# An encoder layer on one core: the issue of two kinds of stores moved from SyncE to GpSimd

## Chip, cores and metric

One Trainium2 chip, one core. The metric is device time in microseconds, the median of three runs of the whole kernel.

## The reference, cut to what matters

One encoder layer is applied to two sequences, of 1024 and 256 tokens, with the same weights. The tokens' projection feeds three groups of heads: a gated delta rule in both directions over chunks of 64 tokens (group A), a retention (group B) and a windowed attention (group C). Their results are gated, joined, projected and normalised. The change lies in group A:

```python
t_mat = jnp.where(strict, a_mat, 0.0) + jnp.eye(CHUNK)
sol = lax.linalg.triangular_solve(t_mat, rhs, left_side=True, lower=True, unit_diagonal=True)
u, w = sol[..., :dv], sol[..., dv:]
...
def step(state, inp):
    u_c, w_c, qk_c, qd_c, kd_c, cd_c = inp
    v_new = u_c - jnp.einsum('bhcd,bhde->bhce', w_c, state)
    o = jnp.einsum('bhcd,bhde->bhce', qd_c, state) + jnp.einsum('bhcs,bhse->bhce', qk_c, v_new)
    state = state * cd_c + jnp.einsum('bhcd,bhce->bhde', kd_c, v_new)
    return state, o
_, o = lax.scan(step, s0, (u, w, qk, q_dec, k_dec, chunk_decay))
```

For each chunk, head and direction a triangular 64 x 64 matrix is inverted, and a scan over the chunks uses the inverse together with the decayed products of queries and keys.

## The kernel before, in words

The 1280 tokens are 10 blocks of 128, or 20 chunks. All products with weights are done in split precision: a float32 value is a high and a low part, and TensorE does three matmuls for each (`dense`, line 86 by its helper).

The work of group A comes in three stages. `prep_stream` goes over the blocks from the last to the first and over both directions `d`, 20 passes in all. A pass loads a small row of decays from `DRD` into `DJ[d]` (line 606, issued by GpSimd), lets TensorE spread it (`sb`), takes exponentials on ScalarE (`ge`), and multiplies on VectorE into two tiles: `at`, the triangular matrix, and `l2`, the three matrices that the scan will use. Both have two buffers. `at` goes to DRAM twice, four transfers into `AGD` (line 631) and one into `ADD_` (line 633); `l2` goes to DRAM with four transfers into `L2D` (one of line 635 for the upper 64 partitions with 2304 B a run, three of line 638 for the lower 64 with 768 B a run; each has 64 x 2 = 128 runs). A small copy on GpSimd (`elc`, line 629) belongs to each pass.

After five blocks `invert(g)` runs, first for g = 1 and, when all blocks are done, for g = 0. It loads the diagonal 32 x 32 blocks of both directions from `AGD` into rows 0 and 1 of the large tile `ot` (line 405), inverts them in place with 61 products and sums on VectorE (the first, over 120 x 2048 elements, needs all that was loaded), sets the diagonals to one (line 427) and stores each direction into `YDD` (line 429): 120 partitions with 32 runs of 128 B each. Both groups use the same two rows of `ot`, so the loads of g = 0 wait until the stores of g = 1 have landed.

`scan_stream` then joins the 32 x 32 blocks to 64 x 64 inverses (`join`: eight of them, five chunks of one direction each; it loads `an` from `ADD_` and `yn` from `YDD`, transposes on VectorE, has two rounds of 32 x 32 matmuls, a product with a mask on GpSimd into `yc`, and a store into `YCD`), and does 20 steps of the scan in both directions (`step`: loads of `l2`, `yc`, `vt` and `kn`, products on GpSimd with beta and with the decay, `sv`). The four joins of g = 1 come first, then two steps, then the four joins of g = 0.

Between all this the products of the other heads are done as filler: `fill` runs the attention stream and the remaining projections beside the scan. The attention begins with a table of positions made by GpSimd (`iota`, line 805, which becomes `bias`), a copy of the queries that ScalarE and GpSimd share (`qh`, line 843), score matmuls into `sb` (two buffers), and a fused sum and maximum on VectorE (`mx`, line 852), which frees the score buffer.

Each engine works through its instructions in order. That order isn't the order of the code: a scheduler sets it from the streams' costs and a timeline of its own, so an edit in one place can move instructions on every engine. SyncE issues all transfers but those of line 265, 374 and 606, which GpSimd issues.

Of the kernel before, what the change touches and what calls it, by code (L numbers as in the profile page):

```python
# [53 lines left out]
def encoder_kernel(ctx: ExitStack, tc: tile.TileContext, I, O, dbg=None, upto=99):  # L54
    nc = tc.nc
    uid = [0]

    def nm(s):
        uid[0] += 1
        return f"{s}_{uid[0]}"  # L60

    def bc(ap, shape):
        return ap.to_broadcast(list(shape))
# [5 lines left out]
    def ps(tag):  # L69
        return psp.tile([128, 512], F32, tag=tag, name=nm(tag))  # L70
# [14 lines left out]
    def mm(out, lhsT, rhs, start=True, stop=True):  # L85
        nc.tensor.matmul(out, lhsT, rhs, start=start, stop=stop)  # L86

    def tt(eng, out, a, b, op):
        eng.tensor_tensor(out=out, in0=a, in1=b, op=op)  # L89
# [30 lines left out]
    ot = big.tile([128, 8, PADW], F32, tag="OT", name="ot")  # L120
# [35 lines left out]
    def acc():  # L156
        wide.append(wide.pop(0))
        return ps(wide[-1])
# [219 lines left out]
    L2D = [[tc.dram_tile([2, 128, 3, 3, 64], F32, name=f"l2d{d}_{b}") for b in range(NB)] for d in range(2)]  # L378
# [3 lines left out]
    YDD = [[tc.dram_tile([120, 32, 32], F32, name=f"yd{d}_{g}") for g in range(2)] for d in range(2)]  # L382
# [5 lines left out]
    T, B = slice(0, 64), slice(64, 128)  # L388
# [11 lines left out]
    IREG = (0, 1)  # L400

    def invert(g):
        for d in range(2):
            with tc.high_priority():
                nc.sync.dma_start(out=ot[0:120, IREG[d], 0:1056].rearrange("p (a b) -> p a b", a=32),
                                  in_=AGD[d][g].rearrange("q c p r x -> (q c p) r x"))

        def two(o0, o1, *dims):

            a = ot[0:120, IREG[0], o0:o0 + 1]  # L410
            return bass.AP(a.tensor, a.offset, [list(a.ap[0]), [(IREG[1] - IREG[0]) * PADW + o1 - o0, 2], *([list(e) for e in dims])])

        y, yd = two(0, 0, (33, 32), (1, 32)), two(32, 32, (0, 32), (33, 32))
        tt(V, y, y, yd, MUL)
        yield 4.2
        for s in range(1, 31):
            na, nb = s, 31 - s
            t3 = two(1056, 1056, (nb, na), (1, nb))

            c = two(s, 33 * (32 - s) + 31 - s, (33, na), (0, nb))  # L420
            r = two(33 * s + s + 1, 33 * (31 - s), (0, na), (1, nb))
            o = two(s + 1, 33 * (32 - s), (33, na), (1, nb))
            tt(V, t3, c, r, MUL)
            tt(V, o, o, t3, ADD)
            if s % 3 == 0:
                yield 2.8
        V.memset(two(0, 0, (34, 32)), 1.0)
        for d in range(2):
            nc.sync.dma_start(out=YDD[d][g], in_=ot[0:120, IREG[d], 0:1056].rearrange("p (a b) -> p a b", a=32)[:, :, 0:32])

    def weave(*run):

# [72 lines left out]
    with tc.tile_pool(name="pa", reuse_waits="tile", bufs=2) as pa:  # L505
# [78 lines left out]
        def prep_stream():  # L584
            for b in reversed(range(NB)):
                tb = slice(b * 128, (b + 1) * 128)
                g3 = []
                for r in range(2):
                    tk = slice(b * 128 + 64 * r, b * 128 + 64 * r + 64)
                    gram = ps("sa")  # L590
                    g3.append(gram[:, 0:384].rearrange("p (q w) -> p q w", q=3))
                    for p in range(3):
                        for h in range(2):
                            rw, o = slice(64 * h, 64 * h + 64), slice(64 - 64 * h, 128 - 64 * h)
                            mm(g3[r][o, p, :].rearrange("p (w t) -> p w t", w=2), kq[rw, p, 0, tk], kq[rw, p, :, tk])
                kt = ps("tr")
                kt3 = kt[:, 0:384].rearrange("p (q w) -> p q w", q=3)
                for p in range(3):
                    nc.tensor.transpose(kt3[:, p, :], kq[:, p, 0, tb], ident)
                kc = pa.tile([128, 2, 3, 64], F32, tag="kc", name=nm("kc"), bufs=1)  # L600
                for r in range(2):
                    for h, rw in ((1, T), (0, B)):
                        S.copy(kc[rw, r], kt3[64 * r:64 * r + 64, :, 64 * h:64 * h + 64])
                for d in range(2):
                    for l in range(2):
                        nc.gpsimd.dma_start(out=DJ[d][2 * l:2 * l + 2], in_=DRD[d][6 * b:6 * b + 6, l].rearrange("n (s t) -> s n t", s=2))
                    ge = pa.tile([128, 2, 2, 3, 64], F32, tag="ge", name=nm("ge"))
                    for i in range(2):
                        pd = ps("sb")
                        mm(pd[:, 0:384], SD[i], DJ[d].rearrange("r n t -> r (n t)"))  # L610
                        if i == 0:
                            for n in range(6):
                                S.activation(out=ge[:, 0, n // 3, n % 3], in_=pd[:, 64 * n:64 * n + 64], func=AF.Exp,
                                             bias=negd[:, d, 2 * b + n // 3, n % 3:n % 3 + 1])
                        else:
                            S.activation(out=ge[:, 1].rearrange("p c q t -> p (c q t)"), in_=pd[:, 0:384], func=AF.Exp)
                    at = pa.tile([128, 2, 3, 2, 33], F32, tag="at", name=nm("at"), bufs=AB)
                    l2 = pa.tile([128, 2, 3, 3, 64], F32, tag="l2", name=nm("l2"))
                    last = 63 if d == 0 else 0
                    gl = ge[:, 0, :, :, last:last + 1]  # L620
                    el = ge[:, 1, :, :, last:last + 1]
                    S.copy(at[:, :, :, :, 32], bc(nbeta[:, d, 2 * b:2 * b + 2, :].unsqueeze(3), [128, 2, 3, 2]))
                    for r in range(2):
                        tt(V, at[:, r, :, :, 0:32], g3[r][:, :, 0:64].rearrange("p q (w t) -> p q w t", w=2),
                           ge[:, 0, r].rearrange("p q (w t) -> p q w t", w=2), MUL)
                        tt(V, l2[:, r, 1], g3[r][:, :, 64:128], ge[:, 0, r], MUL)
                    tt(V, l2[:, :, 2], kc, bc(gl, [128, 2, 3, 64]), MUL)
                    tt(V, l2[:, :, 0], kq[:, :, 1, tb].rearrange("p q (c t) -> p c q t", c=2), ge[:, 1], MUL)
                    G.tensor_copy(elc[:, d, 2 * b:2 * b + 2, :], el.rearrange("p c q t -> p c (q t)"))
                    for q in range(4):  # L630
                        nc.sync.dma_start(out=AGD[d][b // 5][q, 2 * b % 10:2 * b % 10 + 2].rearrange("c p r x -> r (c p) x"),
                                          in_=at[32 * q:32 * q + 32, :, :, q % 2, :].rearrange("r c p x -> r (c p) x"))
                    nc.sync.dma_start(out=ADD_[d][b // 5][2 * b % 10:2 * b % 10 + 2].rearrange("c p q w t -> p c q w t"), in_=at)

                    nc.sync.dma_start(out=L2D[d][b][:, T].rearrange("r p a q t -> p r (a q t)"),
                                      in_=l2[T].rearrange("p r a q t -> p r (a q t)"))
                    for a, a2 in ((0, 1), (1, 0), (2, 2)):
                        nc.sync.dma_start(out=L2D[d][b][:, B, a2].rearrange("r p q t -> p r (q t)"),  # L638
                                          in_=l2[B, :, a].rearrange("p r q t -> p r (q t)"))
                    yield T_PREP / 2  # L640
                if b % 5 == 0:
                    assert "x2" in gone
                    yield from invert(b // 5)


        for _ in spread((10 * T_PREP + 2 * 32.2, prep_stream()), length(PP)):
            pass
# [504 lines left out]
    with tc.tile_pool(name="fw", reuse_waits="tile", bufs=2) as fw:  # L1152
# [21 lines left out]
        for gi in range(2):  # L1174
            c0 = WSEQ[gi][1]
            w = wf.pop()
            for i, b in enumerate(range(NB) if gi else FO):
                tk = slice(b * 128, (b + 1) * 128)
                p = acc()
# [22 lines left out]
        for gi in range(2):  # L1202
# [10 lines left out]
            for b in range(NB):  # L1213
                tk = slice(b * 128, (b + 1) * 128)
                end = gi == 1 and b == NB - 1
                for j, (o, n) in enumerate(((0, 256), (256, 256)) if end else ((0, 512),)):
                    cs = slice(o, o + n)
                    p = acc()
# [50 lines left out]
```

## Time and profile before

| | us |
|---|---|
| median of three runs | 1094.68 (1089.72 to 1098.46) |
| the profiled execution | 1089.4 |
| its span, first to last instruction | 1087.7 |
| TensorE busy | 1012.3 |
| VectorE busy | 626.2 |
| ScalarE busy | 513.4 |
| GpSimd busy | 237.1 |

Between the span and the execution's time lie 1.7 us. Engines are named PE (TensorE; PEld is its loading of weights), DVE (VectorE), ACT (ScalarE), POOL (GpSimd) and SP (SyncE). The time of an instruction that issues a transfer isn't counted as busy. In brackets behind a row stands how long the engine was idle before it and what ended the wait; where several things are waited for, the one that came last by the profile is named, which isn't always the one that mattered.

### The profile page before, as it was taken

Reading aid. Unit: us, or ns where it says so; the run is one execution under the profiler, and the core shown is the slowest. Engines: PE = TensorE matmul, PEld = TensorE weight load, DVE = VectorE, ACT = ScalarE, POOL = GpSimd, SP = SyncE. Lnnn points to the kernel's source line nnn. Section 1 sums busy time; section 2 is a strip of 40 time slices with the busy share of each in tenths; the row PEclk is TensorE's granted clock in tenths of the full one; section 3 lists DMA queues with packets and bytes.
Section 4 is the critical chain, followed back from the end, with each engine's and each line's share of the span. In section 5 each row is a group of like instructions: output and inputs, shape, how many; then the busy total and the mean of one; then the engine's idle time right before and its main releaser. Section 6 shows DMA issues by size and latency. Waiting matters only on the chain.

```text
span 1087.7 us, 20998 instructions
## 1 busy us (share of the span) xinstructions
PE 1012.3 (93%) x7859; PEld 807.6 (74%) x7859; DVE 626.2 (58%) x1303; ACT 513.4 (47%) x1194; POOL 237.1 (22%) x406
## 2 busy tenths in 40 slices
PE   4999999999896799899998999989789999999996
PEld 4768878887785677677776777767567888888885
DVE  6666676754895985555555664575884333412333
ACT  8476779775454554444344322323341121534544
POOL 2001001111212210312323324554451000112311
PEclk9999999999898899999999899989989999999998
DMA  8112112777778336535544434464572530300211
GB/s 258 37 44 69 45 39 58 170 170 180 164 184 173 104 88 131 146 77 137 127 112 109 113 84 116 115 189 113 155 231 65 172 100 1 97 1 10 98 78 77
DMA packets 199071, 120.57 MB, mean 111 GB/s; under 512 B 105906, under 2 KB 180442, under 8 KB 198970
## 3 DMA queue, kind: packets, MB, share of 16 engines
q1 hardware_dynamic: 194074, 118.97, 40.9%
q8 instruction: 62, 1.02, 0.4%
q0 software_dynamic: 4896, 0.27, 0.4%
q14 instruction: 39, 0.32, 0.1%
HBM read 76.26 MB, written 42.91 MB: 110 GB/s over the span
## 4 chain that ended last, share of the span: by engine, by line
PE 72%; DMA 9%; DVE 8%; issue 3%; ACT 3%; SPq 3%; POOL 2%; DVEq 0%; POOLq 0%; ACTq 0%
PE mm L86 42%; PE sa L86 15%; PE sb L86 8%; PE tr L86 4%; DVE ot L984 2%; PE tr L866 1%; DMA xt<-in_x_prompt 1%; DMA ot<-agd 1%; POOL oo L89 1%; DMA oo<-od 1%; DMA agd<-at 1%; DMA raw<-in_w_in 1%; DMA vt<-vtd 1%; PE tr L1191 1%; SPq L638 1%
## 5 line engine op out<-in xcount | busy, mean ns | idle before, releaser
L86 PE MATMUL mm<-xh,whi 128*128 128x512 f32 x720 | 266.7, 370 | 5.0 <-ACT ot L526 1.8
L86 PE MATMUL mm<-xl,whi 128*128 128x512 f32 x720 | 263.3, 366 | 0.0
L86 PE MATMUL mm<-xh,wlo 128*128 128x512 f32 x720 | 263.2, 366 | 0.0
L86 PEld LDWEIGHTS mm<-xh,whi 128*128 128x128 f32 x720 | 138.5, 192 | 30.3 <-ACT ot L526 2.9
L86 PEld LDWEIGHTS mm<-xh,wlo 128*128 128x128 f32 x720 | 138.1, 192 | 22.2 <-issue 1.0
L86 PEld LDWEIGHTS mm<-xl,whi 128*128 128x128 f32 x720 | 138.4, 192 | 20.4 <-issue 0.7
L89 DVE TENSOR_TENSOR ot<-ot 128x1284 f32<-128x1284 f32 (+16 forms) x131 | 85.0, 649 | 28.7 <-ACT ot L102 16.2
L89 DVE TENSOR_TENSOR wlo<-raw,whi 128x1024 fp32r<-128x1024 f32 (+1 forms) x56 | 56.7, 1015 | 39.0 <-ACT whi L149 26.2
L86 PE MATMUL mm<-whi,xh 128*128 128x512 f32 (+1 forms) x168 | 66.6, 398 | 1.3 <-ACT xh L1056 1.3
L86 PE MATMUL mm<-whi,xl 128*128 128x512 f32 (+1 forms) x168 | 66.0, 393 | 0.4 <-DVE xl L89 0.4
L86 PE MATMUL mm<-wlo,xh 128*128 128x512 f32 (+1 forms) x168 | 65.9, 392 | 0.0
L86 PE MATMUL sa<-wlo,xh 128*128 128x512 f32 (+1 forms) x160 | 62.7, 392 | 0.0
L86 PE MATMUL sa<-whi,xl 128*128 128x512 f32 (+1 forms) x160 | 62.6, 391 | 0.0
L86 PE MATMUL sa<-whi,xh 128*128 128x512 f32 (+1 forms) x160 | 62.5, 390 | 0.0
L531 DVE SCALAR_TENSOR_TENSOR ot<-ot,cols 128x1284 f32<-128x1284 f32 x36 | 55.9, 1553 | 0.5
L89 DVE TENSOR_TENSOR sgm<-sb,sgm 128x512 f32<-128x512 f32 (+1 forms) x21 | 14.0, 666 | 72.5 <-ACT sgm L102 60.3
L86 PE MATMUL sa<-sv,l 128*64 128x64 f32 (+1 forms) x912 | 45.8, 234 | 4.2 <-DVE sv L748 3.3
L89 POOL TENSOR_TENSOR sv<-sv,elc 64x192 f32<-64x192 f32 x72 | 41.5, 576 | 37.2 <-PE sa L86 22.2
L86 PEld LDWEIGHTS sa<-sv,l 128*64 128x64 f32 (+1 forms) x912 | 35.5, 141 | 16.0 <-issue 5.1
L89 POOL TENSOR_TENSOR ot<-ot,sgm 128x512 f32<-128x512 f32 x19 | 25.4, 1339 | 99.5 <-DVE sgm L89 98.1
L89 POOL TENSOR_TENSOR vt<-vt,sab 128x192 f32<-128x192 f32 x40 | 21.7, 547 | 115.6 <-DMA vt<-vtd 107.0
L149 ACT CAST whi<-raw 128x1024 fp32r<-128x1024 f32 x30 | 31.5, 1050 | 16.9 <-PE mm L86 10.8
(302 smaller groups left out, 1967.2 us busy)
## 6 DMA issues: line engine op xcount, KB each, us to landing
raw<-in_w_in SPq DMA_DIRECT2D x28, 512.0 KB, 4.3
l<-l2d SPq DMA_DIRECT2D x40, 288.0 KB, 2.9
l2d<-l SPq DMA_DIRECT2D x60, 96.0 KB, 2.8
l2d<-l SPq DMA_DIRECT2D x20, 288.0 KB, 3.7
xt<-in_x_prompt SPq DMA_DIRECT2D x8, 512.0 KB, 6.8
ot<-in_x_prompt SPq DMA_DIRECT2D x8, 512.0 KB
raw<-in_w_pg SPq DMA_DIRECT2D x16, 256.0 KB, 3.1
yp<-ot SPq DMA_DIRECT2D x8, 512.0 KB, 2.6
```

The source lines that it names most:

```text
L86: nc.tensor.matmul(out, lhsT, rhs, start=start, stop=stop)
L89: eng.tensor_tensor(out=out, in0=a, in1=b, op=op)
L149: S.copy(hi, raw)
L531: V.scalar_tensor_tensor(out=Y[:, 0:1284], in0=R[:, j:j + 1284], scalar=cw(ti, j), in1=Y[:, 0:1284], op0=MUL, op1=ADD)
L638: nc.sync.dma_start(out=L2D[d][b][:, B, a2].rearrange("r p q t -> p r (q t)"), in_=l2[B, :, a].rearrange("p r q t -> p r (q t)"))
L866: nc.tensor.transpose(pt[:, k * 128:(k + 1) * 128], pr[:, k * 128:(k + 1) * 128], ident)
L984: V.scalar_tensor_tensor(out=st[r, b2, h], in0=st[r, b, h], scalar=gs[r, 2 * p + h:2 * p + h + 1], in1=kvt[r, b, h], op0=MUL, op1=ADD)
L1191: nc.tensor.transpose(pt[:, k * 128:(k + 1) * 128], hb[:, b, (n * 4 + k) * 128:(n * 4 + k + 1) * 128], ident)
```

## The change

The 80 stores of `l2` into `L2D` and the four stores of the inverses into `YDD` are issued by GpSimd instead of SyncE. What is stored, and when it may be, stays as it was.

```diff
--- before.py
+++ after.py
@@ -426,7 +426,7 @@
                 yield 2.8
         V.memset(two(0, 0, (34, 32)), 1.0)
         for d in range(2):
-            nc.sync.dma_start(out=YDD[d][g], in_=ot[0:120, IREG[d], 0:1056].rearrange("p (a b) -> p a b", a=32)[:, :, 0:32])
+            nc.gpsimd.dma_start(out=YDD[d][g], in_=ot[0:120, IREG[d], 0:1056].rearrange("p (a b) -> p a b", a=32)[:, :, 0:32])
 
     def weave(*run):
 
@@ -632,10 +632,10 @@
                                           in_=at[32 * q:32 * q + 32, :, :, q % 2, :].rearrange("r c p x -> r (c p) x"))
                     nc.sync.dma_start(out=ADD_[d][b // 5][2 * b % 10:2 * b % 10 + 2].rearrange("c p q w t -> p c q w t"), in_=at)
 
-                    nc.sync.dma_start(out=L2D[d][b][:, T].rearrange("r p a q t -> p r (a q t)"),
+                    nc.gpsimd.dma_start(out=L2D[d][b][:, T].rearrange("r p a q t -> p r (a q t)"),
                                       in_=l2[T].rearrange("p r a q t -> p r (a q t)"))
                     for a, a2 in ((0, 1), (1, 0), (2, 2)):
-                        nc.sync.dma_start(out=L2D[d][b][:, B, a2].rearrange("r p q t -> p r (q t)"),
+                        nc.gpsimd.dma_start(out=L2D[d][b][:, B, a2].rearrange("r p q t -> p r (q t)"),
                                           in_=l2[B, :, a].rearrange("p r q t -> p r (q t)"))
                     yield T_PREP / 2
                 if b % 5 == 0:
```

The scheduler's order changes on all engines. At the end of the last pass, GpSimd's queue before (space and -) and now (space and +); `l2d` is `L2D`, `yd` is `YDD`, `iot` is the table of positions and `qh` the queries for the scores:

```order
 L629 COPY elc<-ge_3333 128x6
+L638 DMA l2d_0_387<-l_381_3346 64x2x192 x2
+L635 DMA l2d_0_387<-l_381_3346 64x2x576
+L638 DMA l2d_0_387<-l_381_3346 64x2x192
+L429 DMA yd_1_406<-ot 3840x1x32
+L429 DMA yd_1_408<-ot 3840x1x32
 L805 IOTA iot 128x384
 L843 CAST qh_3775<-ot 64x256 x2
```

The stores of the first group of inverses and the last stores of the scan's matrices now stand ahead of the table and of the queries.

VectorE around the first operation of the second inversion (`ot<-ot 120x2x32x32`), before; `pr`, `mx` are the scores' sums and maxima, `xn` the transpose for the first join:

```order
L89 TENSOR_TENSOR kst_3724<-ot,kst_3724 64x256
L89 TENSOR_TENSOR qlz_3753<-ot,qh_3775 64x256 x2
L89 TENSOR_TENSOR ot<-ot 120x2x32x32
L89 TENSOR_TENSOR sg_3431<-sg_3431,sz_3432 128x256
L852 ISA pr_3785,mx_3772<-sb_3782,bias,snk 128x256
L852 ISA mx_3772 128x1
L852 ISA pr_3792,mx_3772<-sb_3789,bias,snk 128x256
L852 ISA mx_3772 128x1
L682 STREAM_TRANSPOSE xn_445_3901<-yn_3896 128x480
L89 TENSOR_TENSOR ot<-ot 120x2x30
L854 TENSOR_SCALAR mx_3772<-mx_3772 128x1 x2
```

and now, from the third of the four maxima on (the first two stand ahead of these rows):

```order
L852 ISA pr_3799,mx_3772<-sb_3796,bias,snk 128x256
L852 ISA mx_3772 128x1
L852 ISA pr_3806,mx_3772<-sb_3803,bias,snk 128x256
L852 ISA mx_3772 128x1
L89 TENSOR_TENSOR wlo_3577<-raw_3574,whi_3576 128x1024
L854 TENSOR_SCALAR mx_3772<-mx_3772 128x1 x2
L89 TENSOR_TENSOR qlz_3753<-ot,qh_3976 64x256
L89 TENSOR_TENSOR es_3774<-rvb,mx_3772 128x4
L89 TENSOR_TENSOR qlz_3753<-ot,qh_3976 64x256
L89 TENSOR_TENSOR ot<-ot 120x2x32x32
L89 TENSOR_TENSOR den_3773<-den_3773,es_3774 128x4
L682 STREAM_TRANSPOSE xn_445_3901<-yn_3896 128x480
```

All four maxima of the first query block, a weight split (`wlo`) and the low parts of the next queries (`qlz`) stand ahead of the inversion's first operation, which stood ahead of all maxima.

VectorE around the first operation of the first inversion, before; `at` and `l` are the products of a pass into its two tiles:

```order
L89 TENSOR_TENSOR at_2639<-sa_2602,ge_2627 128x6x32
L89 TENSOR_TENSOR l_295_2640<-sa_2602,ge_2627 128x192
L89 TENSOR_TENSOR l_295_2640<-kc_2620,ge_2627 128x2x192
L89 TENSOR_TENSOR at_2639<-sa_2609,ge_2627 128x6x32
L89 TENSOR_TENSOR l_295_2640<-sa_2609,ge_2627 128x192
L89 TENSOR_TENSOR l_295_2640<-kq,ge_2627 128x2x192
L89 TENSOR_TENSOR ot<-ot 120x2x32x32
L89 TENSOR_TENSOR ot<-ot 120x2x30 x2
L89 TENSOR_TENSOR at_2698<-sa_2602,ge_2686 128x6x32
```

and now:

```order
L89 TENSOR_TENSOR at_2639<-sa_2602,ge_2627 128x6x32
L89 TENSOR_TENSOR l_295_2640<-sa_2602,ge_2627 128x192
L89 TENSOR_TENSOR ot<-ot 120x2x32x32
L89 TENSOR_TENSOR at_2639<-sa_2609,ge_2627 128x6x32
L89 TENSOR_TENSOR l_295_2640<-sa_2609,ge_2627 128x192
L89 TENSOR_TENSOR l_295_2640<-kc_2620,ge_2627 128x2x192
L89 TENSOR_TENSOR l_295_2640<-kq,ge_2627 128x2x192
L89 TENSOR_TENSOR ot<-ot 120x2x30 x2
L89 TENSOR_TENSOR ot<-ot 120x2x58
```

The operation now stands in the middle of the products of that pass instead of behind them.

## Rows read from the trace of the kernel before

**Rows 1.** Page part 1: busy time, share of the span, instructions

```profile
PE 1012.3 (93%) x7859; PEld 807.6 (74%) x7859; DVE 626.2 (58%) x1303; ACT 513.4 (47%) x1194; POOL 237.1 (22%) x406
```

**Rows 2.** By stage: length, then busy us (count) of PE, PEld, DVE, ACT, POOL

```profile
170.00:260.00 90.00, 90.00 (x559) 75.17 (x559) 56.22 (x105) 68.84 (x180) 12.49 (x29) 1.00 0.66 151
260.00:276.00 16.00, 11.02 (x65) 8.81 (x63) 8.61 (x16) 5.05 (x20) 2.95 (x6) 0.90 0.74 170
276.00:345.00 69.00, 68.59 (x407) 57.57 (x406) 57.23 (x130) 37.60 (x110) 11.44 (x27) 0.97 0.77 171
345.00:361.00 16.00, 2.93 (x14) 2.75 (x15) 9.10 (x17) 3.75 (x12) 7.71 (x12) 0.59 0.80 202
...
435.00:441.00 6.00, 1.76 (x7) 1.28 (x6) 1.30 (x3) 0.00 (x0) 2.81 (x4) 0.93 0.96 241
```

**Rows 3.** Stores and loads of the scan's matrices: duration min/median/max, first and last start

```profile
L638 SPq DMA_DIRECT2D l2d<-l x60: 574/615/4235, 174.9 to 341.6; - x60
...
DMA to landing us min/median/max: 2.2/3.0/4.4
```

**Rows 4.** The four stores of the inverses, same view

```profile
L429 SPq DMA_DIRECT2D yd<-ot x4: 932/2524/4580, 331.6 to 419.5; - x4
```

**Rows 5.** GpSimd in order of time (start us, us), one row of its loads

```profile
4.93 2.90 POOL L265 DMA_DIRECT2D sd<-onesbd  x6
...
96.19 0.54 POOL L374 DMA_DIRECT2D drd<-dr  x1 [17.22 <-DVE dr L89]
...
328.35 0.45 POOL L805 IOTA iot<- 128x384 int32 x1 [2.21 <-DVE l L89]
328.87 1.27 POOL L843 CAST qh<-ot 64x256 fp32r<-64x256 f32 x2
...
L606 POOL DMA_DIRECT2D dj<-drd x40: 548/548/597, 98.7 to 309.1; - x40
```

**Rows 6.** SyncE's queue in order of time, 331 to 345 us

```profile
331.62 5.63 SPq L429 DMA_DIRECT2D yd<-ot  x2
337.30 4.88 SPq L638 DMA_DIRECT2D l2d<-l  x2
...
342.93 0.59 SPq L405 DMA_DIRECT2D ot<-agd  x1
...
344.07 0.50 SPq L405 DMA_DIRECT2D ot<-agd  x1
```

**Rows 7.** VectorE in order of time, 331 to 360 us

```profile
331.05 0.11 DVE L427 MEMSET ot<- 120x64 f32 x1
335.51 1.23 DVE L89 TENSOR_TENSOR wlo<-raw,whi 128x1024 fp32r<-128x1024 f32 x1 [4.34 <-ACT whi L149]
...
352.09 3.82 DVE L89 TENSOR_TENSOR ot<-ot 120x2048 f32<-120x2048 f32 x1 [6.87 <-DMA an<-ad]
...
357.77 0.47 DVE L852 CUSTOM_DVE_ANT_0 pr<-sb,bias,snk 128x256 f32<-128x256 f32 x1
...
358.58 0.67 DVE L682 STREAM_TRANSPOSE xn<-yn 128x480 f32<-128x480 f32 x1
```

**Rows 8.** TensorE in order of time, 344 to 365 us

```profile
344.45 0.48 PE L86 MATMUL sb<-kst,qh 128*128 128x256 f32 x2
...
358.40 0.55 PE L86 MATMUL sb<-kst,qh 128*128 128x256 f32 x1 [13.07 <-DVE mx L852]
...
363.31 1.14 PE L86 MATMUL sb<-xn,an 32*32 32x32 f32 x60
```

**Rows 9.** SyncE from 418 us, then VectorE at 438 us

```profile
418.52 5.04 SPq L429 DMA_DIRECT2D yd<-ot  x2
423.65 4.35 SPq L477 DMA_DIRECT2D gd<-sg  x1
...
438.59 0.68 DVE L682 STREAM_TRANSPOSE xn<-yn 128x480 f32<-128x480 f32 x1 [4.78 <-DMA yn<-yd]
```

## The prediction

> **What bounds the kernel now.** I read the page's busy shares first: TensorE is busy 1012.3 us of a span of 1087.7 [rows 1], so there are about 75 us in which a faster kernel could be found without less work on TensorE. Then the table by stages, to see where those idle stretches lie around the change [rows 2]. While the scan's matrices are prepared, from 170 to 260 us, TensorE is busy for 90.00 of 90 us, and from 276 to 345 us for 68.59 of 69. Between these stands one hole (11.02 of 16 us busy), behind them a large one (2.93 of 16, 345 to 361 us) and a small one (1.76 of 6, 435 to 441 us). All three lie beside a transfer that the change touches, and these three holes are what the change can shrink or widen.
>
> For the large hole I read SyncE's queue, VectorE and TensorE together. VectorE writes the last element of the first group of inverses at 331.05 + 0.11 = 331.16 us [rows 7]. SyncE issues the two stores of it from 331.62 us, in 5.63 us for the pair, then two of the scan's stores in 4.88 us, and the loads of the second group's matrices at 342.93 and 344.07 us [rows 6]. These loads overwrite rows 0 and 1 of `ot`, which the stores read: they can't go out before the stores have landed. The first operation of the second inversion starts on VectorE at 352.09 us after 6.87 us of idleness, and VectorE works in order, so the maxima of the attention scores stand behind it. TensorE has issued its first scores from 344.45 us, needs the first maximum to free a score buffer, and sits idle for 13.07 us; the matmuls of the first join come at 363.31 us [rows 8].
>
> **What the change does, part by part.** It takes 80 stores of the scan's matrices and 4 of the inverses from SyncE to GpSimd. 60 of the 80 have the row of the view, 615 ns at the median on SyncE, and I charge the other 20 the same [rows 3]: 80 x 0.615 = 49.2 us of issuing, about 2.5 us for each of 20 blocks. GpSimd has the room: 12.49 of 90 us and 11.44 of 69 us busy in this stage [rows 2]. GpSimd's issues in this trace take 548 ns for 12 runs of 256 B (the loads of `dj`), 540 ns for 60 runs of 1 KB (`drd`), and 2.90 / 6 = 483 ns for one row [rows 5]. A store of the scan's matrices has 128 runs; by these rows it costs 0.55 to 0.65 us, so 80 of them cost GpSimd 44 to 52 us of a stage of 175 us. The load of `dj` for a block two or three ahead now stands behind four such stores (2.5 us), and these behind VectorE's last product for them; the 20 blocks issue between 174.9 and 341.6 us [rows 3], 8.3 us apart, so that load still has some two block times in hand. I cost it at 0; without that cover it would be at most 2.5 us a block.
>
> What does the relief of SyncE bring in this stage? Nothing from 170 to 260 and from 276 to 345 us, where TensorE is full [rows 2]. In the hole at 260 to 276 us TensorE waits for VectorE, which waits for the load of the first group's matrices. That load now comes before fewer of SyncE's issues (by three stores, 1.8 us), but VectorE's new order puts the inversion's first operation ahead of four products of the block before, so these wait too. Bounds are 0 and 16 - 11.02 = 5 us; I take 1 us, near 0, since the one shift eats the other.
>
> The Trainium skill (DMA: Bandwidth & Descriptors, Issuing engines are not separate DMA queues) says that issuing from more engines saves only the issuing sequencer's time, since the transfers run on the same DMA engines. The full stretches above agree with it: by that rule alone the sum would be 0, which is the first rival below.
>
> **The stores of the inverses** are the one unknown. Each has 120 x 32 = 3840 runs of 128 B, and no row shows GpSimd issuing anything like it. SyncE needs 0.932 to 4.580 us for one, 2.524 at the median [rows 4]. For GpSimd the lower bound is its flat 0.55 us. For the upper bound I charge all of the `drd` issue to its runs: 0.540 / 60 = 9 ns a run, 34.6 us a store. Between them, the difference of one row (483 ns) and 60 runs (540 ns) is 57 / 59, about 1 ns a run, so 0.5 + 3.8 = 4.3 us a store and 8.6 us a pair. I take this last value: it is the nearest to rows that differ by runs alone, and beside SyncE's 2.5 us it looks sane.
>
> With it the large hole comes out like this. The pair is issued from 331.2 to 339.8 us. SyncE's last store was issued by 337.25 us and freed the load at 344.07, 6.8 us later; a store of the scan lands after 3.0 us at the median [rows 3]. So the second load goes out at 339.8 + 3 to 6.8 = 342.8 to 346.6 us, and I take 345, 1 us later than now. VectorE's first inversion operation can then start at 353.1 instead of 352.09. But VectorE's new order has all four score maxima, one weight split and the copies for the next query ahead of it. The maxima are 0.47 us each and the split 1.23 [rows 7], with the small operations some 4 to 5 us in all, behind scores of 344.45 us and a third pair of them 3 us later: they fill the wait. TensorE gets its score buffers at once and does the 24 matmuls of the next product in the hole rather than behind it. The inversion's first operation ends 3.82 us after its start, at about 357, the transpose for the join takes 0.67 [rows 7], and TensorE's join starts at about 357.6 instead of 363.31: 5.7, so 6 us gained. What is late next is the same load, now for the join instead of the scores. GpSimd's own work behind the pair, the position table (0.45 us) and the copy of the queries (1.27 us) [rows 5], moves from 328 to 340 us and ends at 341.6, before TensorE's scores at 344.45: hidden by 2.8 us. If the pair takes longer than 11.4 us, that cover is gone.
>
> The hole at 435 us: SyncE's pair of stores from 418.52 takes 5.04 us and the next store on SyncE 4.35 us, ahead of the loads for the fourth join; VectorE waits 4.78 us for the last of these [rows 9]. The pair leaves that queue, bounds 0 to 4.2 us of TensorE's time (6 - 1.76), I take 2. Against it, GpSimd is held for 8.6 us there, and the mask product of the third join and the scan's products by beta and by the decay stand behind it: bounds 0 to 8.6, I take 2, as TensorE has the product matmuls meanwhile. Net 0.
>
> Sum: -1 - 6 + 0 = -7 us. The profiled execution took 1089.4 us, so 1082.4; it stands 5.3 us below the median of 1094.68, and on the median's level that is 1087.7. I predict 1087 us.
>
> **Rivals.** First, the transfers are hidden anyway: the holes stay because the load for the second inversion is bounded by the landing of 7680 short runs and not by who issues them, and the maxima that now stand ahead of it are late for another reason. For it speaks that TensorE is full in the stretches around; against it that 13.07 us of idleness hang on the order of one VectorE operation. Then the time stays within 5 us of 1094.7.
>
> Second, slower: GpSimd takes much more per run than I took. The place is the first pair, at 331 us. It decides from the point at which the pair's issue takes 8.6 + 7 = 15.6 us, 2 ns a run. At 4 ns, 15.4 us a store, 31 us a pair, the load goes out at 331.2 + 31 + 3 to 6.8, about 367 instead of 344 us: 23 us later, less 6 for the new order, and the position table and queries that the scores need stand behind it too. The second pair holds GpSimd for 31 us while the scan's first steps wait for its products, for up to 10 us more. That gives +17 to +27, 1112 to 1122 us; at the upper bound of 34.6 us a store it is some 60 us for the first pair alone, above 1150. For it speaks that the profile lists GpSimd's queue as software_dynamic and shows nothing over 60 runs on it; against it that 40 issues of `dj` all take 548 to 597 ns whatever VectorE does at the time [rows 5].
>
> Third, a larger gain: the load goes out earlier, since the scan's last two stores no longer hold SyncE for 4.88 us, the first hole closes (5 us), the last one too (4), and the large one loses 12. That is 21 us: 1074.
>
> **How the numbers follow.** A measurement of this kernel tells about 1% from no change, 10.9 us here. The forecast holds 0.48 with its own range of 1079 to 1092, of which (1083.7 - 1079) / 13 = 0.36 lies beyond 1%, or 0.17; the larger gain has 0.16, hidden anyway 0.15, slower 0.21. So faster by over 1% is 0.17 + 0.16 = 0.33, slower by over 1% 0.21, and within 1% the rest, 0.31 + 0.15 = 0.46. For 8 in 10 the range reaches from 1072, just under the larger gain, to 1115, a third of the way into the slow case at 4 ns a run; the rest of the slow case and the tail of the gain are left out.
>
> **What would show it.** Right: GpSimd's four stores of the inverses at 3 to 6 us each; the second load issued near 345 us; TensorE's wait on the score maxima gone and a shorter wait before the first join's matmuls, which start near 358 us; the stretch from 170 to 260 us still full. Wrong: stores of the inverses of over 8 us on GpSimd, or a `dj` load that TensorE's decay matmuls wait for; either puts new idle time into 276 to 345 us, which is full now.

## The result: 0.6% slower, and the profile after

| | before | after |
|---|---|---|
| median of 20 runs each, us | 1095.14 (1088.16 to 1101.23) | 1101.09 (1097.73 to 1108.07) |
| ratio, 95% interval | | 1.0057 (1.0037 to 1.0078) |
| span of the profiled execution, us | 1087.7 | 1098.2 |
| granted TensorE clock in it | 0.969 | 0.962 |

The forecast was 7 us faster; the change made the kernel 6 us slower. The page's busy line of the changed kernel, for [rows 1]:

```profile
PE 1018.9 (93%) x7859; PEld 812.7 (74%) x7859; DVE 625.0 (57%) x1303; ACT 513.2 (47%) x1194; POOL 290.8 (26%) x490
```

GpSimd has 84 instructions and 53.7 us more (237.1 us and 406 before): its 84 new issues are counted as busy, so the section on the profile before is wrong for GpSimd where it says that no issue is.

Busy time times granted clock is TensorE's work in full-speed us: 1012.3 x 0.969 = 980.9 before and 1018.9 x 0.962 = 980.2 after. So the work is the same, and this product can be compared stage by stage. The changed kernel by stage, columns as in [rows 2], where the first three rows have their counterparts; the last three columns are the granted clock, the busy share of the DMA engines and GB/s:

```profile
170.00:260.00 90.00, 87.32 (x512) 72.25 (x512) 52.43 (x96) 65.01 (x170) 29.93 (x58) 0.96 0.62 140
260.00:276.00 16.00, 14.04 (x87) 11.30 (x85) 4.97 (x12) 6.51 (x23) 8.26 (x14) 1.00 0.92 192
276.00:345.00 69.00, 65.11 (x385) 54.94 (x386) 58.97 (x132) 35.28 (x111) 35.53 (x65) 0.93 0.68 162
345.00:380.00 35.00, 19.90 (x142) 16.80 (x142) 24.49 (x51) 15.66 (x35) 15.31 (x22) 0.76 0.71 158
380.00:450.00 70.00, 68.00 (x641) 54.66 (x639) 48.65 (x98) 34.30 (x68) 8.19 (x7) 1.00 0.42 99
```

and the kernel before in the last two stretches:

```profile
345.00:380.00 35.00, 20.87 (x199) 17.70 (x200) 26.55 (x57) 15.66 (x35) 8.92 (x14) 0.80 0.50 130
380.00:450.00 70.00, 65.38 (x697) 52.30 (x696) 49.10 (x111) 34.68 (x75) 10.66 (x14) 0.98 0.51 122
```

Work done, before and after: 170 to 260 us 90.0 and 83.8; 260 to 345 us 9.9 + 66.5 = 76.4 and 14.0 + 60.6 = 74.6; 345 to 380 us 16.7 and 15.1; 380 to 450 us 64.1 and 68.0. That is -6.2, -1.8, -1.6 and +3.9, together -5.7 us. The two profiles differ by 10.5 us and the medians by 6.0. Behind 450 us the changed kernel makes up 3.7 us by 600 us (146.5 and 142.8 us of work) and loses 7.5 from 800 to 1000 us (190.5 and 198.0), so two profiles don't say which stretch the 6.0 us come from; that needs the experiments; what causes this later loss stays open. Up to 450 us the largest loss lies in the stretch from 170 to 260 us, which was full before and which I had costed at 0.

There TensorE stops twice, at 217 and 219 us (changed kernel, TensorE in order of time):

```profile
216.61 0.40 PE L86 MATMUL mm<-xh,wlo 128*128 128x512 f32 x1
217.88 0.82 PE L86 MATMUL sb<-dj,sd 128*128 128x384 f32 x2 [0.87 <-ACT ge L613]
220.42 0.58 PE L86 MATMUL mm<-xh,whi 128*128 128x256 f32 x1 [1.72 <-ACT sz L473]
```

and the clock falls behind the stop (changed kernel, short stretches, columns as in [rows 2]):

```profile
210.00:217.00 7.00, 7.00 (x38) 5.36 (x34) 1.79 (x2) 4.05 (x12) 2.05 (x4) 1.00 0.91 187
217.00:220.40 3.40, 0.83 (x3) 0.37 (x2) 2.50 (x7) 2.10 (x8) 1.81 (x4) 0.84 0.24 42
220.40:226.00 5.60, 5.52 (x25) 5.22 (x25) 1.28 (x4) 3.39 (x11) 1.91 (x4) 0.50 0.54 138
```

It is 0.50 (1.2 GHz) from 220.4 to 226 us, so 5.52 us of busy time do 2.8 us of work. The stop costs 3.40 - 0.83 = 2.6 us, the clock behind it about as much again.

TensorE waits for ScalarE both times. ScalarE at that place (`ge` are the exponentials, `sz` is the copy of a finished product out of TensorE's output buffer), before:

```profile
212.23 1.35 ACT L613 ACTIVATE ge<-sb,negd 128x64 f32<-128x64 f32 x6
213.43 0.25 ACT L622 COPY at<-nbeta 128x12 f32<-128x12 f32 x1
213.52 0.54 ACT L616 ACTIVATE ge<-sb 128x384 f32<-128x384 f32 x1
213.91 0.46 ACT L102 ACTIVATE ot<-ot 128x256 f32<-128x256 f32 x1
215.70 0.59 ACT L473 COPY sz<-mm 128x512 f32<-128x512 f32 x1 [1.34 <-DVE ot L89]
```

and after:

```profile
215.85 0.21 ACT L622 COPY at<-nbeta 128x12 f32<-128x12 f32 x1 [2.86 <-DMA ad<-at]
216.09 0.31 ACT L613 ACTIVATE ge<-sb,negd 128x64 f32<-128x64 f32 x1
216.31 0.50 ACT L101 ACTIVATE ot<-ot,cols 128x256 f32<-128x256 f32 x1
216.71 1.12 ACT L613 ACTIVATE ge<-sb,negd 128x64 f32<-128x64 f32 x5
217.69 0.52 ACT L616 ACTIVATE ge<-sb 128x384 f32<-128x384 f32 x1
218.06 0.45 ACT L102 ACTIVATE ot<-ot 128x256 f32<-128x256 f32 x1
219.78 0.59 ACT L473 COPY sz<-mm 128x512 f32<-128x512 f32 x1 [1.27 <-DVE ot L89]
```

The copy at line 622 writes a column of betas into the next pass's `at`. Its input was ready long ago; all it waits for is the buffer, from which the store into `ADD_` of two passes earlier still reads. Before, it stood behind the six exponentials of the pass in hand. Now it stands ahead of them and waits 2.86 us, and behind it wait the exponentials, which TensorE's next spread of decays needs out of `sb`. The copy `sz`, which TensorE's next product needs, comes late with them: it waits for a VectorE operation (`ot`) that stands behind the products of the pass, and VectorE idles for these exponentials too. Over the stage this wait has grown, first before, then after (waits of ScalarE, 165 to 345 us: us in total, times, longest):

```profile
ACT at L622 <- DMA ad<-at: 19.1, 10, 4.5
```

```profile
ACT at L622 <- DMA ad<-at: 48.7, 14, 8.9
```

The store itself isn't slower: it lands after 3.8 us at the median, 3.9 before. Five of the 20 copies stand ahead of a pass's exponentials now that stood behind them; they start at 215.85, 223.96, 274.28, 305.35 and 324.08 us.

In the large hole the wait on the score maxima is gone, as forecast, but the join waits instead (changed kernel; GpSimd, SyncE, VectorE and TensorE rows, for [rows 6 to 8]):

```profile
343.22 0.59 POOL L635 DMA_DIRECT2D l2d<-l  x1 [2.75 <-DVE sg L89]
...
344.39 3.50 POOL L429 DMA_DIRECT2D yd<-ot  x2
```

```profile
356.09 0.40 SPq L405 DMA_DIRECT2D ot<-agd  x1
...
360.05 0.34 SPq L405 DMA_DIRECT2D ot<-agd  x1
```

```profile
341.21 0.11 DVE L427 MEMSET ot<- 120x64 f32 x1
...
366.77 3.82 DVE L89 TENSOR_TENSOR ot<-ot 120x2048 f32<-120x2048 f32 x1 [5.53 <-DMA yn<-yd]
...
372.19 0.66 DVE L682 STREAM_TRANSPOSE xn<-yn 128x480 f32<-128x480 f32 x1
```

```profile
372.90 1.33 PE L86 MATMUL sb<-xn,an 32*32 32x32 f32 x42 [15.10 <-DVE xn L682]
```

The second load goes out 18.7 us after VectorE's last write (360.05 - 341.32), against 12.9 before. The pair started 3.1 us after that write (344.39 - 341.32), since it stood behind the scan's last two stores on GpSimd. It took only 3.50 us to issue, but it lands late (line 429, the four stores of the inverses, for [rows 4]; a landing counts from the start of the issue):

```profile
L429 POOL DMA_DIRECT2D yd<-ot x4: 1707/1766/1840, 344.4 to 427.9; - x4
...
DMA to landing us min/median/max: 8.9/10.1/12.7
```

The Trainium skill (Perfetto Trace Analysis, DMA Instruction — SWDGE (GPSIMD)) says that the end which the profiler shows for such a transfer is that of the writing of its descriptors, not of the moving of the data; the rows agree, 1.77 us against 8.9 and more.

### The profile page after: what moved, and what is told of

Its sections match the earlier page's. It is cut to its first block, busy times and chain, and to the rows that moved or that the text cites. A ratio compares the mean times of both kernels' runs of the same rounds, so it can differ in the third digit from the quotient of the medians.

```text
span 1098.2 us, 21063 instructions
## 1 busy us (share of the span) xinstructions
PE 1018.9 (93%) x7859; PEld 812.7 (74%) x7859; DVE 625.0 (57%) x1303; ACT 513.2 (47%) x1194; POOL 290.8 (26%) x490
## 4 chain that ended last, share of the span: by engine, by line
PE 55%; DVE 6%; DMA 5%; SPq 2%; ACT 2%; issue 1%; POOL 1%; DVEq 0%; POOLq 0%; ACTq 0%
PE mm L86 26%; PE sa L86 15%; PE sb L86 7%; PE tr L86 3%; DVE ot L984 2%; DMA yn<-yd 1%; PE tr L866 1%; DVE ot L89 1%; PE tr L1191 1%; DMA an<-ad 1%; DMA ot<-agd 1%; DMA raw<-in_w_out 1%; DVE kd L89 0%; DVE l L89 0%; SPq L678 0%
## 5 line engine op out<-in xcount | busy, mean ns | idle before, releaser
L89 DVE TENSOR_TENSOR ot<-ot 128x1284 f32<-128x1284 f32 (+16 forms) x131 | 81.8, 624 | 27.4 <-ACT ot L102 17.1
L89 DVE TENSOR_TENSOR sgm<-sb,sgm 128x512 f32<-128x512 f32 (+1 forms) x21 | 14.0, 666 | 66.5 <-ACT sgm L102 53.9
L89 POOL TENSOR_TENSOR sv<-sv,elc 64x192 f32<-64x192 f32 x72 | 38.2, 530 | 48.3 <-PE sa L86 23.3
L852 DVE CUSTOM_DVE_ANT_0 pr<-sb,bias,snk 128x384 f32<-128x384 f32 (+1 forms) x40 | 21.7, 562 | 36.5 <-PE sb L86 25.6
```

The lines of the kernel that those rows point to most:

```text
L852: V.tensor_tensor_reduce(out=pr[:, 0:nk * 128], in0=sc[:, 0:nk * 128], in1=bias[:, c0:c0 + nk * 128], scale=1.0, scalar=snk[:, h:h + 1], o ...
```

## Experiments

Theory A: the loss comes with the order that the scheduler makes for the new queues, above all with the copies into `at`. Rival B: the stores on the second queue cost it themselves, by delaying what SyncE moves or GpSimd's loads of `DJ`. Rival C: the stores of the inverses cost it, as they land later. All ratios are to the kernel before, measured beside each run on the same chip (its medians there 1091.6 to 1093.4 us); the quotient of the two medians differs from the ratio by up to 0.2%. Where the order is held to that of before, GpSimd's own is left free, but for x8.

| run | stores on GpSimd | order of the engines | copies, buffers of `at` | median us | ratio (95% interval) |
|---|---|---|---|---|---|
| e1_l2d_only | scan's | scheduler's | 2 | 1100.07 | 1.0080 (1.0052 to 1.0108) |
| e2_yd_only | inverses' | scheduler's | 2 | 1088.80 | 0.9984 (0.9962 to 1.0006) |
| e3_after_ab3 | all | scheduler's | 3 | 1099.37 | 1.0075 (1.0049 to 1.0101) |
| e4_before_ab3 | none | scheduler's | 3 | 1089.80 | 0.9990 (0.9971 to 1.0009) |
| x1_afterq_beforeo | all | of before | 2 | 1087.77 | 0.9950 (0.9931 to 0.9969) |
| x2_beforeq_aftero | none | of after | 2 | 1099.50 | 1.0064 (1.0039 to 1.0089) |
| e5_after_pin | all | scheduler's | all back, 2 | 1093.99 | 1.0004 (0.9985 to 1.0023) |
| e6_before_pin | none | scheduler's | all back, 2 | 1088.84 | 0.9964 (0.9945 to 0.9984) |
| x3_aftero_ab3 | all | of after | 3 | 1089.14 | 0.9973 (0.9953 to 0.9993) |
| x4_beforeo_l2d | scan's | of before | 2 | 1088.46 | 0.9966 (0.9946 to 0.9987) |
| x5_beforeo_yd | inverses' | of before | 2 | 1088.94 | 0.9977 (0.9952 to 1.0002) |
| x6_beforeo_both_ab3 | all | of before | 3 | 1089.76 | 0.9973 (0.9950 to 0.9995) |
| x7_aftero_five_back | all | of after | five back, 2 | 1091.03 | 0.9981 (0.9958 to 1.0003) |
| x8_beforeo_copies_early | none | of before | five ahead, 2 | 1097.19 | 1.0046 (1.0018 to 1.0073) |
| x7_aftero_all_back | all | of after | all back, 2 | 1090.55 | 0.9995 (0.9971 to 1.0020) |
| x9_beforeo_both_copies_back | all | of before | all back, 2 | 1088.49 | 0.9966 (0.9941 to 0.9991) |

**Which stores.** Each half of the change alone; against the changed kernel (e1), and against the kernel before (e2):

```diff
-            nc.gpsimd.dma_start(out=YDD[d][g], in_=ot[0:120, IREG[d], 0:1056].rearrange("p (a b) -> p a b", a=32)[:, :, 0:32])
+            nc.sync.dma_start(out=YDD[d][g], in_=ot[0:120, IREG[d], 0:1056].rearrange("p (a b) -> p a b", a=32)[:, :, 0:32])
```

```diff
-            nc.sync.dma_start(out=YDD[d][g], in_=ot[0:120, IREG[d], 0:1056].rearrange("p (a b) -> p a b", a=32)[:, :, 0:32])
+            nc.gpsimd.dma_start(out=YDD[d][g], in_=ot[0:120, IREG[d], 0:1056].rearrange("p (a b) -> p a b", a=32)[:, :, 0:32])
```

> Only the stores of the scan's matrices go to GpSimd, those of the inverses stay on SyncE. Theory A (ScalarE's copy into `at` now stands ahead of the exponentials of the pass in hand and waits for the store into ADD_): the loss from 170 to 345 us is all here, ScalarE's wait at line 622 is 40 us or more as in the changed kernel (48.7), and the time is 3 to 8 us above the kernel before. Rival C (the loss is the late landing of the inverses' stores, 8.9 us at the median against 2.2 on SyncE): the time is within 2 us of the kernel before.

> Only the stores of the inverses go to GpSimd. Theory A: TensorE stays full from 170 to 260 us, ScalarE's wait at line 622 stays near 19 us as in the kernel before, and the time is within 3 us of it, plus or minus what the holes at 345 and 435 us give. Rival C: the hole at 345 us is 3 us or more longer than before, and the time is 4 us or more above the kernel before.

The scan's stores alone lose 0.80% (8.7 us, a little over the 3 to 8 expected), those of the inverses alone nothing. Rival C falls. (The landings of 8.9 and 2.2 us in the expectation of e1 are not figures of these stores: that view mixed in the loads that read them. On GpSimd the median is 10.1 us; on SyncE the trace has no landing of the stores, only bounds.) A and B both expected this; ScalarE's wait at line 622 is 36.8 us in e1, under the 40 forecast, and 18.9 in e2. The copies stand ahead of the exponentials in e1 at the same places as in the changed kernel, in e2 as in the kernel before: it is the move of the scan's stores that shifts them.

**A third buffer for `at`,** in the changed kernel (e3) and in the kernel before (e4):

```diff
-AB = 2
+AB = 3
```

> The changed kernel with a third buffer for `at`; the order on TensorE, VectorE and GpSimd is that of the changed kernel. Theory A: ScalarE's wait at line 622 falls from 48.7 us to under 10, TensorE is full again from 170 to 230 us, and the time is 5 to 9 us under the changed kernel (1092 to 1096). Rival B (the second ring delays what SyncE issues, whoever waits for it): the wait turns up elsewhere, the time stays within 2 us of the changed kernel.

> The kernel before with a third buffer for `at`, the order as before. Theory A: the wait at line 622 falls from 19.1 us to under 5; as TensorE is full there already, only the hole at 260 us can gain, 0 to 3 us: 1092 to 1095. Rival B: no change, 1094 to 1096.

A miss: nothing changed, the wait is 47.9 us in e3 and 21.1 in e4. The scheduler put each copy one pass further ahead, so that it waits for the same store as with two buffers. This run tells nothing between A and B, since it didn't take the wait away.

**Order against queues.** The scheduler lets an instruction be tied behind another on its engine. A list of the order of one kernel, given as such ties, holds the other kernel to it (x1: TensorE, VectorE, ScalarE and what stays on SyncE; x2: the first three):

```diff
+def pin(tc, orders):
+    live = {i.name: i for i in tc.nc.cur_bb.bb.instructions}
...
+                    tc.add_manual_dep(i, before.name, mybir.DependencyInfo(
+                        mybir.DependencyClass.NoSync, mybir.DependencyReason.DATA), reason="pin")
...
         encoder_kernel(tc, args, outs)
+        pin(tc, ORDER)
```

> The changed kernel's queues with the order of the kernel before: TensorE, VectorE, ScalarE and what stays on SyncE are held to the order of the kernel before, and only the 84 stores are issued by GpSimd, between its own instructions where the scheduler puts them. Theory A (the order that the scheduler makes for the new queues costs the time, above all the copies into `at` that stand ahead of exponentials): TensorE is full from 170 to 260 us and the time is within 3 us of the kernel before. Rival B (the stores on the second queue themselves cost the time: they delay what SyncE moves, or GpSimd's own loads of DJ): the time is 5 to 10 us above the kernel before, as in the changed kernel.

> The converse: all 84 stores on SyncE as in the kernel before, TensorE, VectorE and ScalarE held to the order of the changed kernel. Theory A: the loss is here, 5 to 12 us above the kernel before, with a wait of 40 us or more at line 622. Rival B: within 3 us of the kernel before.

The order costs the time, not the queue. With SyncE's queue and the new order the kernel is 0.64% slower, with GpSimd's queue and the old order 0.50% faster; from 170 to 230 us TensorE is busy 56.46 us in x2 and 60.00 in x1. Rival B falls, and A holds in its wide form. In x2 the wait at line 622 is 37.2 us where 40 were expected. In x1 it is 30.1 us, more than before, and costs nothing that shows there, as the copies stand behind the exponentials. No run holds a kernel to its own order and changes nothing else; that x2, held, and the changed kernel, free, lose about the same (0.64 and 0.57%) is the nearest sign that the ties themselves cost little.

**The copies alone, the scheduler free otherwise** (e5 in the changed kernel, e6 in the kernel before):

```diff
-                    S.copy(at[:, :, :, :, 32], bc(nbeta[:, d, 2 * b:2 * b + 2, :].unsqueeze(3), [128, 2, 3, 2]))
+                    tc.keep_in_program_order(S.copy(at[:, :, :, :, 32], bc(nbeta[:, d, 2 * b:2 * b + 2, :].unsqueeze(3), [128, 2, 3, 2])))
```

> The changed kernel with each copy into `at` held behind the exponentials of its own pass on ScalarE (an edge that orders the issue only); all else is left to the scheduler, which moves much of the order elsewhere too. Theory A in its narrow form (these copies are the cause): ScalarE's wait at line 622 falls from 48.7 us to under 10, TensorE is full from 170 to 230 us, the time is 5 to 9 us under the changed kernel. Wider form (the order as a whole, not these copies): the time can end on either side, the wait at 622 falls but TensorE still has holes before 260 us. Rival B: no change against the changed kernel.

> The same edge in the kernel before. Narrow form of theory A: the wait at line 622 of 19.1 us goes, the hole at 260 us shrinks, 0 to 3 us under the kernel before. Wider form: anywhere within 8 us of it, by the chance of another order.

In e5 the wait at line 622 falls to 0.2 us, the stretch from 170 to 230 us is full (60.00 at a clock of 1.00), and the loss is gone. Both runs gain, 0.5% against the changed kernel and 0.4% against the one before, but the order moved on every engine, so how much of it is due to the copies stays open here.

**The third buffer with the order held, and each half of the change in the old order.** x3 is e3 with every engine held to the order of the changed kernel; x4 and x5 are e1 and e2 held to the order of the kernel before; x6 is x1 with the third buffer.

> The changed kernel, every engine held to its order, with a third buffer for `at`: now a copy waits for a store of a pass further back and stands where it stood. Narrow theory (the copies that stand ahead of exponentials and wait for the store into ADD_ are what this order costs): ScalarE's wait at line 622 falls from 48.7 us to under 10, TensorE is full from 170 to 230 us, and the time is 5 to 8 us under the changed kernel: 0.998 to 1.001 of the kernel before. If the rest of the order costs it: still 1.004 to 1.008.

> The order of the kernel before, only the stores of the scan's matrices on GpSimd. If the 5 us that both moves gain in this order come from these stores (SyncE issues the loads of the first inversion earlier, the hole at 260 us closes by 4 us): 0.995 to 0.997 of the kernel before. If from the stores of the inverses: 0.999 to 1.002.

> The order of the kernel before, only the stores of the inverses on GpSimd. If the scan's stores carry the gain: 0.999 to 1.003, with the load for the second inversion later, as these stores land later from GpSimd. If the stores of the inverses carry it, by freeing SyncE for 10 us: 0.995 to 0.997.

> The order of the kernel before, all 84 stores on GpSimd, and a third buffer for `at` as well: the candidate for a kernel better than both. If the wait of 30.1 us left at line 622 in that order still costs TensorE time: 0.991 to 0.994 of the kernel before. If it is hidden there, as TensorE is full from 170 to 260 us: 0.994 to 0.997, as without the buffer.

In x3 no wait for this store is left (the only one at line 622 is 3.4 us for a store into `AGD`), TensorE is full from 170 to 230 us, and the loss is turned round, from 1.0057 to 0.9973. In the old order the scan's stores gain 3.7 us, those of the inverses 2.5 and both 5.5 (the ratios times 1092), but the interval of x5 reaches 1.0002 and those of x1, x4 and x6 overlap, so the share of each isn't settled (x5 lies between the two ranges expected of it, x3 just below its range and x6 just above). The third buffer adds nothing there.

**Five copies.** A third buffer also frees VectorE's products of `at`. The last runs move copies on ScalarE only, with two buffers and every engine held otherwise (in x9 all but GpSimd). x7_aftero_five_back moves five of the 20, three of which are here, of ScalarE's order in the changed kernel:

```
 L100 ACTIVATE ot<-sz_2266 128x256
-L622 COPY at_1809<-nbeta 128x12
 L613 ACTIVATE ge_1737<-sb_1738,negd 128x64
 L101 ACTIVATE ot<-ot,cols 128x256
 L613 ACTIVATE ge_1737<-sb_1738,negd 128x64 x5
+L622 COPY at_1809<-nbeta 128x12
...
-L622 COPY at_1938<-nbeta 128x12
 L102 ACTIVATE ot<-ot 128x512
 L613 ACTIVATE ge_1797<-sb_1798,negd 128x64 x6
+L622 COPY at_1938<-nbeta 128x12
...
+L613 ACTIVATE ge_2627<-sb_2628,negd 128x64 x6
 L622 COPY at_2698<-nbeta 128x12
-L613 ACTIVATE ge_2627<-sb_2628,negd 128x64 x6
```

x8 moves the same five the other way in the kernel before; x7_aftero_all_back and x9 put all 20 behind the exponentials of their own pass, in the changed kernel's order and in x1.

> The changed kernel with every engine held to its order, but for five copies into `at` on ScalarE, which stand behind a pass's exponentials as in the kernel before instead of ahead of them. If these copies cost the time: TensorE full from 170 to 230 us, 0.997 to 1.001 of the kernel before. If the third buffer helped in another way: 1.004 to 1.008 as in the changed kernel.

> The kernel before with every engine held to its order, but for the same five copies, put ahead of the pass's exponentials as in the changed kernel; all stores on SyncE. If these copies cost the time: 1.003 to 1.009 of the kernel before, TensorE no longer full from 170 to 230 us. If not: 0.998 to 1.002.

> The changed kernel held to its order, with all 20 copies into `at` behind the exponentials of their own pass. If the other 15 cost something there too: 1 to 4 us under the run with five moved. If the five are all: the same within 2 us.

> The order of the kernel before, all 84 stores on GpSimd, and all 20 copies behind the exponentials of their own pass: the other candidate for a kernel better than both. If copies still cost time in that order: 0.991 to 0.994 of the kernel before. If not: 0.994 to 0.998, as without that move.

Five copies of 0.2 us each are the loss against the kernel before. Moved back, they take the changed kernel from 1.0057 to 0.9981; moved ahead, they take the kernel before to 1.0046, with none of its stores on another queue. TensorE is busy 58.68 us of 60 from 170 to 230 us at a clock of 1.00 with them back, 57.75 with them ahead, where it was full. ScalarE in x8, at the place shown of the other two kernels:

```profile
216.42 0.72 ACT L101 ACTIVATE ot<-ot,cols 128x512 f32<-128x512 f32 x1
219.85 0.21 ACT L622 COPY at<-nbeta 128x12 f32<-128x12 f32 x1 [2.71 <-DMA ad<-at]
219.96 0.92 ACT L613 ACTIVATE ge<-sb,negd 128x64 f32<-128x64 f32 x4
```

and in x7_aftero_five_back:

```profile
212.38 0.32 ACT L613 ACTIVATE ge<-sb,negd 128x64 f32<-128x64 f32 x1
212.59 0.50 ACT L101 ACTIVATE ot<-ot,cols 128x256 f32<-128x256 f32 x1
212.99 1.12 ACT L613 ACTIVATE ge<-sb,negd 128x64 f32<-128x64 f32 x5
215.66 0.21 ACT L622 COPY at<-nbeta 128x12 f32<-128x12 f32 x1 [1.55 <-DMA ad<-at]
```

The copy waits in both; only in x8 do exponentials stand behind it, and there TensorE stops for VectorE, which needs them:

```profile
221.47 0.87 PE L86 MATMUL sa<-kq 64*64 64x128 f32 x12 [2.25 <-DVE l L89]
```

The granted clock stays at 1.00 from 170 to 345 us in x8, so the lower clock of the changed kernel doesn't follow every such stop. TensorE's waits in these 175 us come to 10.8 us in x8 and 5.3 before, but the clock fell behind the hole at 270 us before (0.53 from 275 to 280 us) and not in x8: in work x8 is 2 us behind at 345 us, and how its 5 us come together one profile doesn't settle. The sum of ScalarE's waits at line 622 in x7_aftero_five_back shows how little the sum says:

```profile
ACT at L622 <- DMA ad<-at: 43.8, 13, 11.2
```

It is 43.8 us, near the 48.7 of the changed kernel, and the kernel is 8 us faster, no slower within the intervals than x3, which has none of these waits. The other 15 copies cost nothing measurable in either order. Whether the new order costs something beyond the copies stays open: with them back it stands at 0.9981 and 0.9995, and x1, with the old order and the same queues, at 0.9950, with intervals that overlap for the first and just miss for the second.

The best is x1, 0.50% below the kernel before. e6, x4 and x9 (0.34 to 0.36% below) beat it and the changed kernel too, and can't be told from x1.

## Why the prediction was wrong

**The step that failed** is "Nothing from 170 to 260 and from 276 to 345 us, where TensorE is full". A full stretch has nothing to gain, but it has something to lose. I had named the order as able to move instructions on every engine, and looked at what it moved only around the two inversions, on GpSimd and VectorE. ScalarE's order in the full stretch, by which TensorE was kept full, I didn't read; five copies there cost about 8 us by x7 (0.0057 + 0.0019 of the time) and 5 by x8 (0.0046). That was none of my rivals: the slower case was put on GpSimd's time per run. Neither of my two signs of being wrong came, no store of over 8 us on GpSimd and no wait for `DJ`; what failed was the sign of being right that these 90 us stay full.

**The rest of the sum.** x1, which has the queues without the new order, gained 0.0031 to 0.0069 of 1092.6 us, 3.4 to 7.5 us, and -7 was forecast. That the two agree is luck: 6 of my 7 us were to come from the new order, with the score maxima ahead of the inversion, and x1 keeps the old one. TensorE still waits there as it did [rows 8]:

```profile
353.42 0.55 PE L86 MATMUL sb<-kst,qh 128*128 128x256 f32 x1 [11.33 <-DVE mx L852]
```

Where x1's gain comes from isn't settled. The terms one by one:

- The scan's stores on GpSimd, 0.55 to 0.65 us: right, 0.592 us for the upper ones and 0.610 for the others at the median. That the loads of `DJ` stay hidden: right, no wait of TensorE on them shows.
- The stores of the inverses, 4.3 us each to issue: 1.77 us. The slow rival fell with that, 3.5 us a pair against its 15.6. But behind the end of the issue I took 3 to 6.8 us to the landing, from SyncE's queue, and it is 7.1 to 10.9 (8.9 and 12.7, less 1.77). My 6.8 was a bound and not a landing: SyncE issues without a gap of more than 0.13 us from 331.62 us to the load at 344.07, so its queue may have held that load. The 3.0 is of a view that has the loads in it; line 638 alone has 2.8. From VectorE's last write to the second load I had 345 - 331.2 = 13.8 us; it was 18.7 in the changed kernel and 15.2 in x1 (341.9 - 326.7). Of the 18.7 us 3.1 are the late start of the pair, 3.5 its issue and 12.2 what comes behind, where I had 0, 8.6 and 5.2.
- The large hole, -6: the wait of 13.07 us on the maxima went [rows 8], as the new order has them ahead. The join came 31.6 us after VectorE's last write (372.90 - 341.32), where I had 26.4 (357.6 - 331.2) and before it was 32.1 (363.31 - 331.16). So the gain there is 0.5 us, as the late load ate the rest; what I had named as late next, the load, was it.
- The hole at 435 us, 0: the stretch from 380 to 450 us did 3.9 us more work in the changed kernel. I had put GpSimd's hold at 8.6 us against it, and the pair holds GpSimd for 3.4.
- The hole at 260 us, -1 within 0 and 5: from 260 to 345 us the changed kernel did 1.8 us less work, so a loss and out of the bounds. In the order of the kernel before, single profiles give 13.0 of 16 us busy in x1, 11.5 in x4 and 10.5 in x6, against 11.0, so what the queue alone does there isn't settled.

The rule of the Trainium skill (DMA: Bandwidth & Descriptors, Issuing engines are not separate DMA queues), by which only the issuing sequencer's time is saved, was the first rival, which I put at 0. x1 stands 5 us below it with the work unchanged, and the stores became slower to land, not faster. The issue time saved on SyncE is what is left to explain it, and the rule allows that; it isn't shown, as GpSimd's order was free in x1. That the full stretches agree with the rule, as I wrote, was no evidence: TensorE was full there whoever issued.

Why the scheduler moves the copies ahead was not tried. That they go ahead in e1 and not in e2, and one pass further with a third buffer, would fit a timeline in which the store into `ADD_`, with fewer issues around it on SyncE, has landed sooner than it does on the chip, but no run shows this.

## What to carry to other kernels

Where a scheduler sets the order, a change of a queue is also a change of every engine's order, so read the new order first where the bounding engine is full, and look for an instruction that waits for nothing but a buffer and now stands ahead of work on the critical path. To tell order from queue, hold one kernel to the other's order: two runs settled here what six with a free scheduler left open. Judge a wait by what stands behind it on its engine and not by its length: 43.8 us of waits cost nothing measurable here, and one of 2.86 us, with the stop and the lower clock behind it, cost more than 5 in the changed kernel's profile.

## What the runs showed of the hardware

- A store of 3840 runs of 128 B takes GpSimd 1.71 to 1.88 us to issue and lands 8.7 to 15.4 us from the start of it (over all runs that issue it there; 8.9 to 12.7 in the changed kernel, up to 15.4 in e5). SyncE takes 0.89 to 5.6 us to issue it (e1), and what stands right behind a pair takes another 4.4 to 4.9 us (4.35 in [rows 9], 4.88 for two transfers in [rows 6]); yet the load that waits for the second store went out at most 8.1 us after its start in x2 (352.48 - 344.38). So the engine that was quicker to issue was not the one that had the data there sooner.
- The scan's stores land later from GpSimd too: 3.6 us at the median for line 638 (2.8 on SyncE) and 4.4 for line 635 (3.7), in the changed kernel and the one before.
- A stop of 2.6 us on TensorE was followed by 5.6 us at a granted clock of 0.50, in which a matmul of 128 x 256 takes 0.41 us instead of 0.28 (the changed kernel, at 221 and at 354 us). No term of my sum had the clock in it; here it doubled the price of the stop, and in x8 a stop of 2.25 us had no such stretch behind it.
